# Second shift of the adaLN modulation without GpSimd: half of it on VectorE, half as modulation pieces on TensorE

## Chip, core and metric

One core of a Trainium2 chip. The time is device microseconds of one execution. TensorE, VectorE, ScalarE and GpSimd each run their own queue of instructions in order; SP (SyncE) issues most of the DMAs. TensorE's clock has two levels, 1.2 and 2.4 GHz; the profile gives the granted clock of a stretch as a share of the higher one.

## What is computed

One layer of a hybrid diffusion backbone on 384 tokens (128 context, 256 latent), D = 2048, everything in float32. What matters here is the modulation: six vectors per stream out of one condition vector each.

```python
sh1, sc1, g1, sh2, sc2, g2 = split(silu(cond) @ w_mod + b_mod, 6)   # cond: c_ctx and c
h = x * (1 + sc1) + sh1
# attention (q, k, v), Conformer convolution (width 31, then LayerNorm), Mamba-2 scan; all out of h @ w_in
x = layer_norm(ALPHA * x + g1 * (concat(A, B, C) @ w_out))
h2 = x * (1 + sc2) + sh2
x = layer_norm(ALPHA * x + g2 * conv_ffn(h2))
```

The second shift `sh2` is a product of a 2 x 2048 matrix with a 2048 x 2048 part of `w_mod`, 16.8 MB. It is needed only after the first LayerNorm.

## The kernel before

Each large matmul runs as three products of a high and a low part. `wpiece` (L219) takes a 512 KB weight piece into ring `raw` (4 buffers), casts its high part on ScalarE (L229) and subtracts for the low part on VectorE (L230). `load` (L213) issues from SP's queue. Instructions with a high priority are placed ahead by the scheduler, but each engine's queue stays in order.

The run has stages. Up to about 220 us: the first modulation and the first part of the input projection. Then a stage whose TensorE order is written out by hand: `phase_zd`, `phase_v`, eight head pairs of `qk_tile`, and the first 512 columns of the output projection (`wo_group` with 0). A planner, `flow`, interleaves small generators with these main matmuls. It keeps a clock of its own, in units meant as microseconds: main matmuls advance it through `tick`; a generator yields two numbers, how far its own TensorE work advances the clock, and after which pause it is due again. `tick` also issues taps of the width-31 convolution on VectorE from a list (`flow.bg`), as many as `flow.rate` times the main units pay for, 0.63 units each. When the main matmuls need a result that no generator has reported as ready, `advance` sets the planner's clock to the next generator's due time, so that no main matmul is issued in between.

The generators: `tok_gen`, `dt_gen` and `ssm_gen` (the scan), `attn_gen` (attention: scores, softmax on VectorE and ScalarE, transposes at L717, values), `conv_ln_gen` (LayerNorm behind the convolution, when the taps are done), `mod2_gen` (first gate and second scale: 64 pieces of 512 KB into ring `v`, 3 buffers, four matmuls of 32 output rows each into one PSUM bank, in batches of three with a pause of 11.5), and `sh2_gen` (second shift, one piece every 9 units from the end of the scan on).

A piece of the second shift (`sh2_piece`, L845) loads 512 KB into ring `raw`, the transposed weights with the output channel on the partition. There are 32 pieces, four quarters of K (`kq`) times eight pairs of output blocks. Odd ones go to `dve_gemv`: one VectorE instruction per half piece and stream multiplies with the broadcast condition row and accumulates. Even ones go to `pool_gemv`: GpSimd multiplies (L842) and ScalarE's copy accumulates (L843). At each new quarter `cond_rows` has GpSimd's queue issue two broadcast loads.

Behind the hand-ordered stage, the output projection's columns 1 to 3 run (three calls of `wo_group`); after each weight piece `sh2_piece` is called until all 32 are done. `mix_rows` and `gate` issue residual rows and gates from GpSimd's queue; `mix_evac` (L925) reads PSUM on VectorE and so frees it. `sh2_end` sums the partial sums in `macc` into `h2b`; the first LayerNorm `ln1` reads them. Then the FFN follows.

Of the kernel before, what the change touches and what calls it, by code (L numbers as in the profile page):

```python
# [15 lines left out]
KC = 16  # L16
# [83 lines left out]
def _build(tc, ctx, a):  # L100
# [112 lines left out]
    def load(src, n, raw=None):  # L213
        raw = raw_t() if raw is None else raw
        with tc.high_priority(offset=HP):
            nc.sync.dma_start(out=raw[:, :n], in_=src)
        return raw
# [250 lines left out]
    def dt_gen():  # L468
        e, u, d, m = s_t(48), s_t(48), s_t(48), s_t(48)
        V.scalar_tensor_tensor(out=e, in0=dtr, scalar=-1.0, in1=dtr, op0=ALU.mult, op1=ALU.min)  # L470
        S.activation(out=e, in_=e, func=AF.Exp)
        V.tensor_scalar_add(out=u, in0=e, scalar1=1.0)
        V.tensor_scalar_add(out=d, in0=u, scalar1=-1.0)
        V.tensor_scalar(out=m, in0=d, scalar1=0.0, scalar2=None, op0=ALU.is_equal)
        V.tensor_tensor(out=d, in0=d, in1=m, op=ALU.add)
        V.reciprocal(out=d, in_=d)
        S.activation(out=u, in_=u, func=AF.Ln)
        V.tensor_tensor(out=u, in0=u, in1=d, op=ALU.mult)
        V.tensor_tensor(out=u, in0=u, in1=m, op=ALU.add)
        V.tensor_tensor(out=u, in0=u, in1=e, op=ALU.mult)  # L480
        V.scalar_tensor_tensor(out=dtv, in0=dtr, scalar=0.0, in1=u, op0=ALU.max, op1=ALU.add)
        ea = s_t(16)
        S.activation(out=ea, in_=P_("a_log", 0, 16), func=AF.Exp)
        V.tensor_scalar(out=ea, in0=ea, scalar1=-1.0, scalar2=None, op0=ALU.mult)
        V.tensor_tensor(out=dA.rearrange("p (c d) -> p c d", c=3), in0=dtv.rearrange("p (c d) -> p c d", c=3),
                        in1=bc(ea, 1, 3), op=ALU.mult)
        yield 0.0, 9.0
        ps = at_t()
        dAv = dA.rearrange("p (c d h) -> p c d h", c=3, d=2)
        csv = cs.rearrange("p (c d h) -> p c d h", c=3, d=2)  # L490
        for d_, tri in ((0, tri_f), (1, tri_b)):
            PE.matmul(ps[:, 32 * d_:32 * d_ + 24], tri, dAv[:, :, d_, :])
            V.tensor_copy(out=csv[:, :, d_, :], in_=ps[:, 32 * d_:32 * d_ + 24].rearrange("p (c h) -> p c h", c=3))
        yield 0.5, 2.0
        PE.matmul(ps[:, 64:112], ones, dA)
        pt = at_t()
        PE.transpose(pt[:48, :128], cs, ident)
        ct = sbt([128, 128], "o", 1)
        V.tensor_copy(out=ct[:48, :], in_=pt[:48, :128])
        G.dma_start(out=csd, in_=ct[:48, :])  # L500
        V.tensor_scalar(out=ncs, in0=cs, scalar1=-1.0, scalar2=None, op0=ALU.mult)
        S.activation(out=eT, in_=ps[:, 64:112], func=AF.Exp)
        V.tensor_tensor(out=dec, in0=ps[:, 64:112], in1=cs, op=ALU.subtract)
        S.activation(out=dec, in_=dec, func=AF.Exp)
        S.activation(out=ecs, in_=cs, func=AF.Exp)
        yield 0.3, 0.0
        ready.add("dt")
# [251 lines left out]
    def mod2_start(g):  # L759
        gS[g] = gm_t()  # L760

    def mod2_load(i):
        g, half, k = i // 32, i // 16 % 2, i % 16
        return load(a["wm2"][g, half, k], 1024, v_t().rearrange("p a b -> p (a b)"))

    def mod2_piece(i, raw):
        g, half, k = i // 32, i // 16 % 2, i % 16
        for j in range(4):
            PE.matmul(gS[g][32 * j:32 * j + 32, 256 * half:256 * half + 256], cond[:, k, :],
                      raw[:, 256 * j:256 * j + 256], start=k == 0, stop=k == KC - 1)  # L770

    gd = {}
    s2 = sbt([128, KC, 2], "s2", 1)
# [2 lines left out]
    def mod2_end(g):  # L776
        ps = gS.pop(g)
        sm = gb_t()[:, :512]
        if g == 0:
            bg = gb_t()[:, :512]  # L780
            pinned(bg, a["bgate"])
            with tc.high_priority(offset=HP):
                V.tensor_tensor(out=sm, in0=ps, in1=bg, op=ALU.add)
            gd[g] = dr.tile([2, D], F32, tag=f"gd{g}", name=nm("gd"))
            for j in range(4):
                G.dma_start(out=gd[g][:, 512 * j:512 * j + 512], in_=sm[32 * j:32 * j + 2, :])
            return
        V.tensor_copy(out=sm, in_=ps)
        yield 0.0, 2.0
        pt = at_t()  # L790
        for b in range(4):
            PE.transpose(pt[:, 128 * b:128 * b + 128], sm[:, 128 * b:128 * b + 128], ident)
        pv = pt.rearrange("p (b j c) -> p j b c", b=4, j=4)[:, :, :, 0:2]
        V.tensor_tensor(out=s2.rearrange("p (j b) c -> p j b c", j=4), in0=pv,
                        in1=bc(b2p.rearrange("p (j b) -> p j b", j=4), 3, 2), op=ALU.add)
        yield 0.5, 1.0

    def mod2_gen(most, gap):
        i = 0
        while i < 64:  # L800
            n = min(most, 32 - i % 32)
            raws = [mod2_load(j) for j in range(i, i + n)]
            yield 0.0, gap
            if i % 32 == 0:
                mod2_start(i // 32)
            for j, raw in enumerate(raws):
                mod2_piece(i + j, raw)
            i += n
            yield 0.45 + 0.43 * n, 0.0
            if i % 32 == 0:  # L810
                yield from mod2_end(i // 32 - 1)

    macc = sbt([128, 32, 4], "macc", 1)
    cbc = []
# [19 lines left out]
        for e in range(2):  # L834
            dve_gemv(raw[:, 512 * e:512 * e + 512], 2 * pr + e, kq)

    sh2_done = [0]

    def pool_gemv(w, kt, kq):
        for s in range(2):  # L840
            j = m_t()
            G.tensor_tensor(out=j, in0=w, in1=cbc[s], op=ALU.mult)  # L842
            S.activation(out=j, in_=j, func=AF.Copy, accum_out=macc[:, 16 * s + kt, kq:kq + 1])  # L843

    def sh2_piece():  # L845
        i = sh2_done[0]
        if i == 32:
            return
        sh2_done[0] += 1
        kq, pr = i // 8, i % 8  # L850
        if pr == 0:
            cond_rows(kq, m_t)
        raw = load(a["wsh2"][kq, pr], 1024)
        for e in range(2):
            (dve_gemv if i % 2 else pool_gemv)(raw[:, 512 * e:512 * e + 512], 2 * pr + e, kq)

    def sh2_gen(gap):
        while "ssm" not in ready:
            yield 0.0, 1.0
        while "stop" not in ready:  # L860
            sh2_piece()
            yield 0.0, gap

    def sh2_end():
        m = s_t(32)
        V.tensor_reduce(out=m, in_=macc, axis=AX.X, op=ALU.add)
        V.tensor_tensor(out=h2b.rearrange("p k s -> p s k"), in0=m.rearrange("p (s k) -> p s k", s=2),
                        in1=bc(P_("bsh2", 0, 16), 1, 2), op=ALU.add)

    def g2_end():  # L870
        m = s_t(32)
# [90 lines left out]
    with tc.manual_schedule(engines={mybir.EngineType.PE}):  # L962
        for i in range(8):
            do_conv5(i)
        for i in range(4):
            flow.bg += conv31_steps(i)
        flow.rate = 0.7
        flow.add(30.0, tok_gen())
        flow.add(0.0, mod2_gen(3, 11.5))
        flow.add(40.0, conv_ln_gen())  # L970
        flow.add(30.0, ssm_gen())
        flow.add(50.0, attn_gen())
        flow.add(60.0, sh2_gen(9.0))
        phase_zd()
        flow.add(0.0, dt_gen())
        phase_v()
        for hp in range(8):
            k = qk_tile(0, hp)
            qk[hp] = (qk_tile(1, hp), k)
        ps = [mm_t() for _ in range(3)]  # L980
        for k in ORDER[:12]:
            cat_split(k)
        wo_group(0, ps, cat_split, lambda last: flow.tick(2.09))
        ready.add("stop")
        flow.drain()
        gb = mix_rows(0)
        for t in range(3):
            mix_evac(t, 0, 0, 512, ps[t], gb)
# [47 lines left out]
    for cg in range(1, 4):  # L1036
        gb = mix_rows(cg)
        ps = [ps_t() for _ in range(3)]
        wo_group(cg, ps, lambda k: None, lambda last: sh2_piece() if last else None)
        for t in range(3):  # L1040
            mix_evac(t, cg, 0, 512 if cg < 3 else 256, ps[t], gb)
    sh2_end()
    LW = 256
    lhi = [t_t(LW, F32R) for _ in range(KC)]
# [179 lines left out]
def _layout(i):  # L1224
# [3 lines left out]
    d = {}  # L1228
# [8 lines left out]
    for q, (k0, nk) in enumerate(PARTS):  # L1237
        w1 = wm[:, :, [1, 0], 128 * k0:128 * (k0 + nk)]
        kpl = 4 // nk
        d[f"wm1_{q}"] = f(w1.reshape(KC // kpl, kpl, 128, 256 * nk).transpose(0, 2, 1, 3).reshape(KC // kpl, 128, 1024))  # L1240
    d["wm2"] = f(wm[:, :, [2, 4]].reshape(KC, 128, 2, 4, 2, 256).transpose(2, 4, 0, 1, 3, 5).reshape(2, 2, KC, 128, 1024))
    for n, c in (("wsh2", 3), ("wg2", 5)):
        g2 = i["w_mod"][0][:, c * D:(c + 1) * D].T.reshape(8, 2, 128, 4, 512)
        d[n] = f(g2.transpose(3, 0, 2, 1, 4).reshape(4, 8, 128, 1024))
# [75 lines left out]
```

## Time and profile before

| | us |
|---|---|
| median of 3 runs | 1890.98 (1887.93 to 1893.52) |
| the profiled execution | 1888.23, span 1886.5 |
| TensorE busy | 1811.3 |
| VectorE busy | 1186.7 |
| ScalarE busy | 816.1 |
| GpSimd busy | 148.9 |
| mean granted TensorE clock | 0.985 |

TensorE is busy for 96% of the span. Idle time of another engine costs nothing by itself; what counts is what ended an idle stretch of TensorE, and whom that engine had waited for in turn. Times are counted from the span's start.

### The profile page before, as it was taken

Reading aid. Unit: us, or ns where it says so; the run is one execution under the profiler, and the core shown is the slowest. Engines: PE = TensorE matmul, PEld = TensorE weight load, DVE = VectorE, ACT = ScalarE, POOL = GpSimd, SP = SyncE. Lnnn points to the kernel's source line nnn. Section 1 sums busy time; section 2 is a strip of 40 time slices with the busy share of each in tenths; the row PEclk is TensorE's granted clock in tenths of the full one; section 3 lists DMA queues with packets and bytes.
Section 4 is the critical chain, followed back from the end, with each engine's and each line's share of the span. In section 5 each row is a group of like instructions: output and inputs, shape, how many; then the busy total and the mean of one; then the engine's idle time right before and its main releaser. Section 6 shows DMA issues by size and latency. Waiting matters only on the chain. (4 is left out here: it accounts for less than half of the span.)

```text
span 1886.5 us, 28860 instructions
## 1 busy us (share of the span) xinstructions
PE 1811.3 (96%) x10794; PEld 1635.4 (87%) x10794; DVE 1186.7 (63%) x2457; ACT 816.1 (43%) x1606; POOL 148.9 (8%) x213
## 2 busy tenths in 40 slices
PE   8999999989989888999999999999999999999998
PEld 6888988768776667999988999988999988999987
DVE  3865899944454567666743666744666644667567
ACT  4223543665655445644433444432444432444434
POOL 0000001110323452000000000000000000000000
PEclk9999999999989999999999999999999999999999
DMA  8898467656655765244444455444544544454354
GB/s 316 309 323 287 148 224 248 210 185 206 235 203 179 232 197 203 90 140 140 151 134 131 149 169 166 157 124 130 171 157 147 167 123 130 156 167 151 118 147 144
DMA packets 108652, 337.76 MB, mean 179 GB/s; under 512 B 12584, under 2 KB 17160, under 8 KB 108512
## 3 DMA queue, kind: packets, MB, share of 16 engines
q1 hardware_dynamic: 101280, 311.65, 50.5%
q0 software_dynamic: 7232, 24.28, 4.3%
q8 instruction: 84, 1.38, 0.3%
q14 instruction: 56, 0.46, 0.1%
HBM read 331.08 MB, written 4.79 MB: 178 GB/s over the span
## 5 line engine op out<-in xcount | busy, mean ns | idle before, releaser
L230 DVE TENSOR_TENSOR wlo<-raw,whi 128x512 fp32r<-128x512 f32 (+1 forms) x755 | 528.0, 701 | 483.2 <-ACT whi L229 476.1
L229 ACT CAST whi<-raw 128x512 fp32r<-128x512 f32 (+1 forms) x755 | 466.4, 620 | 843.2 <-PE mm L455 303.3
L454 PE MATMUL mm<-hl,whi 128*128 128x384 f32 x1245 | 429.0, 345 | 1.4 <-ACT whi L229 1.1
L455 PE MATMUL mm<-hl,whi 128*128 128x384 f32 x1245 | 422.6, 339 | 0.0
L456 PE MATMUL mm<-hl,wlo 128*128 128x384 f32 x1245 | 421.7, 339 | 0.0
L454 PEld LDWEIGHTS mm<-hl,whi 128*128 128x128 f32 x1245 | 236.0, 190 | 11.9 <-issue 5.7
L455 PEld LDWEIGHTS mm<-hl,whi 128*128 128x128 f32 x1245 | 236.1, 190 | 0.6 <-DVE wlo L230 0.2
L456 PEld LDWEIGHTS mm<-hl,wlo 128*128 128x128 f32 x1245 | 236.1, 190 | 0.0
L454 PE MATMUL sc<-hl,whi 128*128 128x384 f32 x659 | 222.8, 338 | 0.0
L455 PE MATMUL sc<-hl,whi 128*128 128x384 f32 x659 | 221.9, 337 | 0.0
L456 PE MATMUL sc<-hl,wlo 128*128 128x384 f32 x659 | 221.7, 336 | 0.0
L454 PEld LDWEIGHTS sc<-hl,whi 128*128 128x128 f32 x659 | 123.6, 188 | 2.9 <-ACT whi L229 1.6
L455 PEld LDWEIGHTS sc<-hl,whi 128*128 128x128 f32 x659 | 123.7, 188 | 0.1
L456 PEld LDWEIGHTS sc<-hl,wlo 128*128 128x128 f32 x659 | 123.7, 188 | 0.0
L826 DVE SCALAR_TENSOR_TENSOR junk<-raw,gb 128x512 bf16<-128x512 f32 x128 | 87.6, 684 | 50.2 <-DMA raw<-wg 50.1
L448 PE MATMUL mm<-whi,hl 128*128 128x512 f32 (+2 forms) x293 | 104.1, 355 | 7.7 <-DVE g L925 4.8
L449 PE MATMUL mm<-wlo,hl 128*128 128x512 f32 (+2 forms) x293 | 101.8, 347 | 2.3 <-DVE wlo L230 2.3
L450 PE MATMUL mm<-whi,hl 128*128 128x512 f32 (+2 forms) x293 | 101.3, 346 | 0.0
L842 POOL TENSOR_TENSOR m<-raw,m 128x512 f32<-128x512 f32 x64 | 86.7, 1383 | 117.9 <-DMA raw<-wsh 94.4
L450 PE MATMUL mm<-whi,t 128*128 128x512 f32 (+1 forms) x232 | 89.7, 387 | 0.0
L449 PE MATMUL mm<-wlo,t 128*128 128x512 f32 (+1 forms) x232 | 89.6, 386 | 0.0
L448 PE MATMUL mm<-whi,t 128*128 128x512 f32 (+1 forms) x232 | 89.5, 386 | 0.0
(354 smaller groups left out, 2592.6 us busy)
## 6 DMA issues: line engine op xcount, KB each, us to landing
raw<-wu SPq DMA_DIRECT2D x176, 512.0 KB, 3.5
raw<-wd SPq DMA_DIRECT2D x79, 512.0 KB, 3.7
m<-wm SPq DMA_DIRECT2D x128, 256.0 KB, 5.6
v<-wm SPq DMA_DIRECT2D x64, 512.0 KB, 6.1
raw<-wA SPq DMA_DIRECT2D x32, 512.0 KB, 5.5
raw<-wqk SPq DMA_DIRECT2D x32, 512.0 KB, 4.2
raw<-wsh SPq DMA_DIRECT2D x32, 512.0 KB, 4.3
raw<-wo SPq DMA_DIRECT2D x32, 512.0 KB, 4.4
```

The costliest lines, as they stand in the source:

```text
L229: S.copy(out=hi[:, :w], in_=rw)
L230: V.tensor_tensor(out=lo[:, :w], in0=rw, in1=hi[:, :w].bitcast(F32), op=ALU.subtract)
L448: PE.matmul(ps[:, :n], A, hi[:, w0:w0 + n], start=k == 0, stop=False)
L449: PE.matmul(ps[:, :n], A, lo[:, w0:w0 + n], start=False, stop=False)
L450: PE.matmul(ps[:, :n], B, hi[:, w0:w0 + n], start=False, stop=k == last)
L454: PE.matmul(ps[:, :T], A, hh[k], start=k == k0, stop=False)
L455: PE.matmul(ps[:, :T], A, hl[k], start=False, stop=False)
L456: PE.matmul(ps[:, :T], B, hh[k], start=False, stop=k == k1)
L826: V.scalar_tensor_tensor(out=j, in0=w, scalar=1.0, in1=cbc[s], op0=ALU.mult, op1=ALU.mult, accum_out=macc[:, 16 * s + kt, kq:kq + 1])
L842: G.tensor_tensor(out=j, in0=w, in1=cbc[s], op=ALU.mult)
```

## The change

The second shift's first half of K (quarters 0 and 1) stays on VectorE, in 32 steps of one output block and one quarter each: `sh2_load` takes 256 KB into ring `m`, and the condition rows with the first of a quarter; `sh2_step` computes the step at the head of a queue and issues the next load. Three loads are issued before the first step. The second half of K becomes 16 more pieces of `mod2_gen` (a third accumulation group, `wm3`), whose end writes `h2b` with the bias; `sh2_end` adds VectorE's half. GpSimd's products and ScalarE's accumulating copies are gone. Four numbers of the planner change: the pause of `mod2_gen` from 11.5 to 9, that of the second shift from 9 to 4 per step, `dt_gen`'s first pause from 9 to 14, and the taps' rate from 0.7 to 0.45.

```diff
-        yield 0.0, 9.0
+        yield 0.0, 14.0
...
+    def mod2_of(i):
+        return (i // 32, i // 16 % 2, i % 16, 0) if i < 64 else (2, (i - 64) // 8, 8 + i % 8, 8)
     def mod2_load(i):
-        g, half, k = i // 32, i // 16 % 2, i % 16
-        return load(a["wm2"][g, half, k], 1024, v_t().rearrange("p a b -> p (a b)"))
+        g, half, k, _ = mod2_of(i)
+        src = a["wm2"][g, half, k] if g < 2 else a["wm3"][half, k - 8]
+        return load(src, 1024, v_t().rearrange("p a b -> p (a b)"))
...
-        V.tensor_tensor(out=s2.rearrange("p (j b) c -> p j b c", j=4), in0=pv,
-                        in1=bc(b2p.rearrange("p (j b) -> p j b", j=4), 3, 2), op=ALU.add)
+        dst, bias = (s2, b2p) if g == 1 else (h2b, P_("bsh2", 0, 16))
+        V.tensor_tensor(out=dst.rearrange("p (j b) c -> p j b c", j=4), in0=pv,
+                        in1=bc(bias.rearrange("p (j b) -> p j b", j=4), 3, 2), op=ALU.add)
...
-        while i < 64:
-            n = min(most, 32 - i % 32)
+        while i < 80:
+            n = min(most, 32 - i % 32, 80 - i)
...
-    def pool_gemv(w, kt, kq):
-        for s in range(2):
-            j = m_t()
-            G.tensor_tensor(out=j, in0=w, in1=cbc[s], op=ALU.mult)
-            S.activation(out=j, in_=j, func=AF.Copy, accum_out=macc[:, 16 * s + kt, kq:kq + 1])
...
-        raw = load(a["wsh2"][kq, pr], 1024)
-        for e in range(2):
-            (dve_gemv if i % 2 else pool_gemv)(raw[:, 512 * e:512 * e + 512], 2 * pr + e, kq)
+    def sh2_load():
+        i = sh2_n[0]
+        if i == 32:
+            return
+        sh2_n[0] += 1
+        kq, kt = i // 16, i % 16
+        w = m_t()
+        with tc.high_priority(offset=HP):
+            nc.sync.dma_start(out=w, in_=a["wsh2"][kq, kt // 2, :, 512 * (kt % 2):512 * (kt % 2) + 512])
+        rows = None
+        if kt == 0:
+            rows = [m_t() for _ in range(2)]
+            for s in range(2):
+                G.dma_start(out=rows[s], in_=crow[s:s + 1, 512 * kq:512 * kq + 512].to_broadcast([128, 512]))
+        sh2_q.append((w, kt, kq, rows))
+
+    def sh2_step():
+        if sh2_q:
+            w, kt, kq, rows = sh2_q.pop(0)
+            if rows:
+                cbc[:] = rows
+            dve_gemv(w, kt, kq)
+        sh2_load()
...
+        for _ in range(3):
+            sh2_load()
+            yield 0.0, gap
         while "stop" not in ready:
-            sh2_piece()
+            sh2_step()
             yield 0.0, gap
...
-        flow.rate = 0.7
+        flow.rate = 0.45
-        flow.add(0.0, mod2_gen(3, 11.5))
+        flow.add(0.0, mod2_gen(3, 9.0))
-        flow.add(60.0, sh2_gen(9.0))
+        flow.add(60.0, sh2_gen(4.0))
...
-        wo_group(cg, ps, lambda k: None, lambda last: sh2_piece() if last else None)
+        wo_group(cg, ps, lambda k: None, lambda last: sh2_step() if last else None)
...
+    while sh2_q:
+        sh2_step()
     sh2_end()
```

## Rows read from the trace of the kernel before

**Rows 1.** The page, busy time: engine, us, share of the span, instructions.

```profile
PE 1811.3 (96%) x10794; PEld 1635.4 (87%) x10794; DVE 1186.7 (63%) x2457; ACT 816.1 (43%) x1606; POOL 148.9 (8%) x213
```

**Rows 2.** By stretch: length, PE, PEld, DVE, ACT, POOL busy, granted clock, DMA share, GB/s.

```profile
190.00:780.00 590.00, 532.54 (x3443) 451.90 (x3442) 404.38 (x864) 318.13 (x755) 131.50 (x162) 0.96 0.60 199
```

**Rows 3.** TensorE's waits, 270:290 us: who for whom, sum in us, times, longest.

```profile
PE at L492 <- issue: 3.4, 1, 3.4
PE at L492 <- DVE cs L493: 0.3, 1, 0.3
```

**Rows 4.** TensorE's waits, 480:545 us.

```profile
PE at L717 <- ACT p L707: 4.5, 3, 2.7
PE at L717 <- ACT t L603: 3.3, 1, 3.3
```

**Rows 5.** TensorE's waits, 600:630 us.

```profile
PE at L717 <- ACT t L733: 4.8, 2, 2.6
PE at L717 <- ACT p L707: 2.6, 2, 1.9
```

**Rows 6.** TensorE's waits, 650:741 us, the four largest.

```profile
PE mm L448 <- DVE g L925: 4.8, 1, 4.8
PE sc L448 <- DVE g L925: 3.6, 1, 3.6
PE mm L448 <- ACT whi L229: 2.7, 2, 1.5
PE mm L449 <- DVE wlo L230: 2.3, 4, 1.6
```

**Rows 7.** By stretch, columns as in rows 2.

```profile
280.00:300.00 20.00, 18.74 (x95) 14.65 (x96) 17.96 (x39) 5.02 (x11) 1.09 (x2) 0.91 0.52 172
600.00:640.00 40.00, 32.60 (x145) 23.46 (x144) 21.08 (x45) 18.93 (x47) 19.32 (x24) 0.87 0.71 224
700.00:720.00 20.00, 13.38 (x55) 10.73 (x54) 11.74 (x23) 9.51 (x23) 10.32 (x10) 0.83 0.59 202
```

**Rows 8.** In order of time, 658:670 us (four engines); last, ScalarE's wait, 460:740.

```profile
661.51 5.11 POOL L842 TENSOR_TENSOR m<-raw,m 128x512 f32<-128x512 f32 x4 [4.93 <-DMA raw<-wsh]
666.05 0.60 ACT L229 CAST whi<-raw 128x512 fp32r<-128x512 f32 x1
666.68 0.69 DVE L230 TENSOR_TENSOR wlo<-raw,whi 128x512 fp32r<-128x512 f32 x1 [4.95 <-ACT whi L229]
667.90 0.69 DVE L925 TENSOR_TENSOR g<-sc,gb 128x512 f32<-128x512 f32 x1
668.64 0.80 PE L448 MATMUL sc<-whi,hl 128*128 128x512 f32 x1 [3.56 <-DVE g L925]
...
ACT m L843 <- POOL m L842: 53.8, 40, 4.4
```

**Rows 9.** Groups of TensorE by line, 190:600 us: busy, mean ns, idle before.

```profile
L769 PE MATMUL gm<-v,cond 128*32 128x256 f32 x512 | 32.2, 383 | 0.0
L792 PE MATMUL at<-cons,gb 128*128 128x128 f32 x4 | 0.7, 286 | 1.4 <-DVE gb L788 1.4
```

**Rows 10.** Tile v's landing; SP's issue of one batch; a TensorE wait, whole span.

```profile
DMA to landing us min/median/max: 3.6/6.1/9.8
448.14 1.37 SPq L216 DMA_DIRECT2D v<-wm  x3
PE gm L280 <- DMA m<-wm: 7.7, 4, 4.4
```

**Rows 11.** By stretch, columns as in rows 2.

```profile
260.00:380.00 120.00, 112.49 (x756) 93.60 (x754) 113.53 (x230) 60.04 (x143) 13.53 (x22) 0.99 0.65 223
380.00:460.00 80.00, 71.69 (x488) 59.90 (x484) 37.52 (x79) 50.09 (x120) 9.69 (x17) 0.94 0.55 181
300.00:400.00 100.00, 94.91 (x671) 80.32 (x669) 84.31 (x165) 52.70 (x134) 16.12 (x27) 1.00 0.68 230
```

**Rows 12.** TensorE's waits, 400:470 us.

```profile
PE at L717 <- ACT p L707: 7.1, 2, 4.7
```

More of the change, by code (lines that the diff above doesn't have):

```diff
@@ L760, in mod2_start @@
         gS[g] = gm_t()
+    def mod2_of(i):
+        return (i // 32, i // 16 % 2, i % 16, 0) if i < 64 else (2, (i - 64) // 8, 8 + i % 8, 8)
     def mod2_load(i):
-        g, half, k = i // 32, i // 16 % 2, i % 16
-        return load(a["wm2"][g, half, k], 1024, v_t().rearrange("p a b -> p (a b)"))
+        g, half, k, _ = mod2_of(i)
+        src = a["wm2"][g, half, k] if g < 2 else a["wm3"][half, k - 8]
+        return load(src, 1024, v_t().rearrange("p a b -> p (a b)"))
     def mod2_piece(i, raw):
-        g, half, k = i // 32, i // 16 % 2, i % 16
+        g, half, k, k0 = mod2_of(i)
         for j in range(4):
             PE.matmul(gS[g][32 * j:32 * j + 32, 256 * half:256 * half + 256], cond[:, k, :],
-                      raw[:, 256 * j:256 * j + 256], start=k == 0, stop=k == KC - 1)
+                      raw[:, 256 * j:256 * j + 256], start=k == k0, stop=k == KC - 1)
     gd = {}
@@ L809, in mod2_gen @@
             yield 0.45 + 0.43 * n, 0.0
-            if i % 32 == 0:
-                yield from mod2_end(i // 32 - 1)
+            if i in (32, 64, 80):
+                yield from mod2_end((i - 1) // 32)
     macc = sbt([128, 32, 4], "macc", 1)
@@ L835, in g2_piece @@
             dve_gemv(raw[:, 512 * e:512 * e + 512], 2 * pr + e, kq)
-    sh2_done = [0]
-    def pool_gemv(w, kt, kq):
-        for s in range(2):
-            j = m_t()
-            G.tensor_tensor(out=j, in0=w, in1=cbc[s], op=ALU.mult)
-            S.activation(out=j, in_=j, func=AF.Copy, accum_out=macc[:, 16 * s + kt, kq:kq + 1])
-    def sh2_piece():
-        i = sh2_done[0]
+    sh2_q = []
+    sh2_n = [0]
+    def sh2_load():
+        i = sh2_n[0]
         if i == 32:
             return
[L849 to L852, printed above, removed]
-        raw = load(a["wsh2"][kq, pr], 1024)
-        for e in range(2):
-            (dve_gemv if i % 2 else pool_gemv)(raw[:, 512 * e:512 * e + 512], 2 * pr + e, kq)
+        sh2_n[0] += 1
[16 more added lines that the diff above has]
+        sh2_load()
     def sh2_gen(gap):
@@ L865, in sh2_end @@
         m = s_t(32)
-        V.tensor_reduce(out=m, in_=macc, axis=AX.X, op=ALU.add)
-        V.tensor_tensor(out=h2b.rearrange("p k s -> p s k"), in0=m.rearrange("p (s k) -> p s k", s=2),
-                        in1=bc(P_("bsh2", 0, 16), 1, 2), op=ALU.add)
+        V.tensor_reduce(out=m, in_=macc[:, :, 0:2], axis=AX.X, op=ALU.add)
+        hp_ = h2b.rearrange("p k s -> p s k")
+        V.tensor_tensor(out=hp_, in0=hp_, in1=m.rearrange("p (s k) -> p s k", s=2), op=ALU.add)
     def g2_end():
@@ L1241, in _layout @@
     d["wm2"] = f(wm[:, :, [2, 4]].reshape(KC, 128, 2, 4, 2, 256).transpose(2, 4, 0, 1, 3, 5).reshape(2, 2, KC, 128, 1024))
+    d["wm3"] = f(wm[8:, :, 3].reshape(8, 128, 4, 2, 256).transpose(3, 0, 1, 2, 4).reshape(2, 8, 128, 1024))
     for n, c in (("wsh2", 3), ("wg2", 5)):
```

## Prediction, made before the changed kernel was run

> **What bounds the kernel now.** I read the page first, then the waits of TensorE, then single stalls in order of time. TensorE is busy 1811.3 of 1886.5 us [rows 1], so only two things can move the end: matmul work, and TensorE's idle time with the clock that it costs. The 75 us of idle time don't lie evenly. The up and down projections from about 780 us on run at full width; most of it lies between 190 and 780 us, in the hand-ordered stage and the output projection: TensorE is busy there for 532.6 of 590 us, at a mean clock of 0.96 [rows 2]. There the listing in order of time and the waits by stretch show four clusters that the change can reach: 3.4 and 0.3 us where the dt matmul comes [rows 3]; 3.3 and 4.5 us at attention transposes between 480 and 545 us [rows 4]; 4.8 and 2.6 us at the last attention step, 600 to 630 us [rows 5]; 4.8, 3.6, 2.7 and 2.3 us in output columns 1 to 3, 650 to 741 us [rows 6]. Behind these stalls the granted clock falls below 1.00: 0.91 in the 20 us behind the first (and as much behind the second and behind the 3.6 us of the fourth), 0.87 over 40 us around the third, 0.83 around the 4.8 us of the fourth [rows 7]. A mean of 0.91 over 20 us is a part of the stretch at 1.2 instead of 2.4 GHz; it costs 0.09 x 20 = 1.8 us of full-speed work. I count it as a part of the stall.
>
> What makes the stalls of the fourth cluster is seen in one chain [rows 8]: GpSimd starts four products of the second shift at 661.51 us, when their tile has landed; ScalarE's accumulating copies stand in its queue behind them, so the weight's high part is cast only at 666.05; VectorE's low part follows at 666.68 and the eviction that frees the PSUM bank at 667.90; TensorE starts again at 668.64, 3.6 us late. Over the stage ScalarE stood 53.8 us before these copies, 40 times [rows 8]. The engines have room; their queues are in order, and one late tile holds three of them.
>
> **Parts that take time away.** (a) dt_gen's pause grows from 9 to 14 planner units (one unit is meant as 1 us). The planner puts 5 us more main matmuls ahead of the dt matmul, against 3.7 us of waiting, and the taps ahead of the dt chain on VectorE become sparser. I take the whole: 3.7 + 1.8 of clock = 5.5 us; bounds 0 and 5.5.
>
> (b) and (d) GpSimd's 64 products and ScalarE's 64 copies go. VectorE keeps 64 products (32 steps x 2 streams, before 16 pieces x 4), but in single steps, on tiles requested three steps earlier, out of ring m and no longer out of ring raw, which also holds every weight piece. So the queue chain above has no first link, and the weight loads behind a raw tile that GpSimd held are free too. For (b), 480 to 545 us, 3.3 + 4.5 + 1.8 of clock = 9.6 us; bounds 3 and 9.6, since an attention transpose also waits for exponentials that stay. For (d), 4.8 + 3.6 + 2.7 + 2.3 = 13.4, with 0.09 x 20 + 0.17 x 20 = 5.2 of clock, is 18.6; I leave 1.6 for refilling at three group starts and take 17; bounds 8 and 18.6. The planner's own additions say how much second shift reaches this place: before, 12 of 32 pieces are issued in the ordered stage and 20 in the three groups (8 + 8 + 4); after, with a pause of 4 for 9, 21 of 32 steps come earlier, 8 lie in the first group, 3 in the second, none in the third.
>
> (c) The last attention step. Adding up the planner's units: main matmuls are 32 x 1.09 + 16 x 2.09 + 256 x 0.522 + 16 x 2.09 = 235.4, and before, they reach head pair 7 at unit 350.7 while its attention ends at 357.5; the planner jumps ahead with nothing to issue. The trace has that as 7.4 us of idle and 0.13 x 40 = 5.2 of clock [rows 5, 7], 12.6 in all. After, the 16 new pieces push the main matmuls back and attention 7 ends at 354.2 with 10 units of output projection left, so something is there to issue. I take 10, since waits for single exponentials stay; bounds 3 and 12.6.
>
> Together 5.5 + 9.6 + 17 + 10 = 42.1 us.
>
> **Parts that add.** (e) 16 pieces on TensorE: the 64 pieces now take 32.2 us of engine time [rows 9], so 16 x 32.2 / 64 = 8.05 us, on the path, since TensorE is the bound. (f) One more mod2_end: four transposes, 0.7 us, and by the existing one a wait of 1.4 us for VectorE's copy [rows 9]: 2.1 us. Its two VectorE instructions and the one addition in sh2_end lie beside matmuls. (g) Denser modulation: batches of three come after a pause of 9 instead of 11.5, and there are 28 instead of 22. All three v buffers are in use, so a batch's load is issued only when the previous batch's matmuls have run. It lands 6.1 us after issue in the median, 9.8 at worst, and the third load is issued about 1 us after the first [rows 10]; by its additions the planner leaves 9.3 to 10.9 units. So most are hidden and the worst come about 1 us late: 2 us, bounds 0 and 34 (below). These loads stand on SP's queue, and weight loads behind one that waits for its buffer wait too; against that, ring raw holds four pieces.
>
> (h) The taps' rate falls from 0.7 to 0.45. By the planner the last tap comes at unit 272 instead of 154, so VectorE is less crowded than its 113.5 of 120 us at first and more than its 37.5 of 80 us later [rows 11]: 124 taps of 0.63 units over 272 units add 29%, about 76% in all. What crowding costs is bounded by the stretch where it is worst: TensorE idles 5.1 us in 300 to 400 us [rows 11]. At 0.64 of the density, over 118 units more, 5.1 / 100 x 118 x 0.64 = 3.9, less 1.8 at the first place. I take 4; bounds 0 and 8. The last tap meets the second shift's first step at unit 266, so the two crowds hardly overlap. The conv LayerNorm moves with the taps; its stall of 7.1 us at 416 us [rows 12] I move unchanged.
>
> GpSimd's queue keeps only DMA issues: the four row broadcasts (eight before), the biases, gates and residual rows no longer stand behind products. SP issues as many bytes as before, 32 loads of 256 KB and 16 of 512 KB instead of 32 of 512 KB. A load of 512 KB lands in 9.8 us at worst [rows 10]; three steps ahead is 12 units or more, so I cost these at nothing. If that cover failed, VectorE would stand before them in its queue, with splits and evictions behind it, and every us of it would reach TensorE as in the chain above.
>
> The Trainium skill speaks against this split: its page "DMA: Bandwidth & Descriptors", section "Bandwidth", wants transfers of 1 MiB or more, and its fixed 2.0 us plus bytes / 436 GB/s makes an estimated 2.6 us of 256 KB and 3.2 us of 512 KB, so 32 x 2.6 + 16 x 3.2 - 32 x 3.2 = 32 us more of queue occupancy. By the rows that occupancy is hidden and the sum keeps its value; by the page alone it could be at most those 32 us later.
>
> Sum: 8.05 + 2.1 + 2 + 4 = 16.2 added, 42.1 taken away, net -25.9. Against the profiled execution, 1888.23 us with a span of 1886.5, that is 1862.3; the median of the runs is 1890.98, 2.75 above it, so I forecast **1865 us**.
>
> **Rivals.** R1, slower: the modulation's v loads become the bound. In the first modulation TensorE did wait for such loads, 7.7 us in 4 waits [rows 10]. If the third load of each batch lands as late as the worst one now, 1.0 + 9.8 against 9.6 units of usable pause, 28 batches lose some 1.2 us each, 34 us, and the time is 1899. It decides once landing passes about 8.6 us after issue in the typical batch. Against it: not one of the 22 batches now waited [rows 9]. R2: the taps and the LayerNorm, moved among the steps of the second shift and attention, stall TensorE twice, 7.1 us once more and (h) at 8: 1865 + 11 = 1876. For it: that stage's exponentials already come last in most of its waits. R3, the change doesn't free what it means to free: behind the copies the weight loads, or the exponentials themselves, are late anyway, and half of (b), (c) and (d) stays: 18.3 us, 1883. For it: the casts also wait for landing weights now; against it, these weights share their ring and queue with the tiles that GpSimd holds.
>
> **How the numbers follow.** Chances: forecast 0.57, R2 0.17, R3 0.11, R1 0.15. With every bound at its best end (46.3 taken, 8.8 added, and the LayerNorm's 7.1 gone) the time is 1846; the upper end leaves out most of R1: 1846 to 1890. A measurement of this kernel tells about 0.3%, 5.7 us, from no change. Faster by more: forecast, R2 and part of R3, 0.77; within: 0.10; slower: 0.13.
>
> **What would show it.** Right: no idle time of TensorE ended by evictions in output columns 1 to 3, ScalarE with no wait for GpSimd, granted clock 1.00 from 600 to 720 us, the dt stall gone, the modulation's matmuls up by 8 us, none of them behind a DMA. Wrong: waits for v tiles (R1); attention transposes idle for ScalarE's exponentials between 400 and 600 us in sum more than now (R2); casts waiting for weights in the output groups (R3).

## The result and the profile after

| | before | after |
|---|---|---|
| median, us | 1889.45 (1887.25 to 1893.52) | 1834.11 (1833.33 to 1837.13) |
| profiled span, us | 1886.5 | 1835.3 |
| TensorE idle in the span, us | 75.2 | 36.0 |
| mean granted clock | 0.985 | 0.994 |

The ratio is 0.9708, 95% interval 0.9686 to 0.9729: 55 us less, where 1865 was forecast and 1846 was the lower end of the range. The direction was right, the size less than half of what came, and the time lies outside the range.

Cut the run at four places that both kernels have: the last evacuation of `phase_zd`, the last query tile, the first eviction of the output projection, the first cast of the LayerNorm's result. First the kernel before, then after; columns as in rows 2.

```profile
264.80:566.10 301.30, 273.41 (x1859) 229.53 (x1858) 198.15 (x426) 170.24 (x424) 54.46 (x69) 0.95 0.63 212
566.10:629.80 63.70, 55.00 (x305) 39.44 (x304) 29.20 (x72) 34.31 (x91) 25.41 (x29) 0.92 0.60 189
629.80:753.20 123.40, 105.28 (x552) 87.71 (x551) 86.76 (x185) 55.91 (x132) 49.98 (x42) 0.96 0.65 212
```

```profile
264.70:561.30 296.60, 279.85 (x2013) 231.50 (x2011) 227.76 (x532) 165.41 (x402) 30.91 (x51) 0.97 0.75 261
561.30:603.90 42.60, 42.60 (x251) 32.12 (x250) 17.88 (x40) 20.39 (x49) 7.95 (x15) 1.00 0.66 205
603.90:702.80 98.90, 98.90 (x561) 86.04 (x560) 58.75 (x111) 35.67 (x69) 3.75 (x7) 1.00 0.52 156
```

The value, key and query stage is 4.7 us shorter, the last attention step with the first output columns 21.1, the other output columns 24.5. What lies behind took 1133.3 and 1132.5 us, what lies ahead 264.8 and 264.7. The second and third stretch now have no idle time of TensorE at all and a clock of 1.00; where rows 5 and 6 showed 7.4 us and 13.4 us of listed waits there is nothing left. The second stretch is not the same work before and after: some of its main matmuls and attention now lie in the first.

In the first stretch waits remain, and not fewer where I had expected that. TensorE's waits, 474 to 548 us, after (answers to rows 4):

```profile
PE at L717 <- ACT p L707: 4.8, 3, 3.2
PE at L717 <- ACT t L603: 0.9, 1, 0.9
PE at L599 <- DVE m L595: 0.6, 1, 0.6
PE at L717 <- ACT pt L719: 0.6, 1, 0.6
PE at L717 <- ACT g L385: 0.4, 1, 0.4
```

They sum to 7.3 us, against 7.8 in rows 4. The next two answers suggest why; no run tests it alone: the second shift's products on VectorE (ns min/median/max, first and last start), and a stretch in which VectorE is nearly full (columns as in rows 2).

```profile
L831 DVE SCALAR_TENSOR_TENSOR junk<-m,m x64: 671/691/694, 474.6 to 547.3; 128x512 bf16<-128x512 f32 x64
```

```profile
500.00:540.00 40.00, 35.05 (x235) 27.09 (x235) 38.58 (x108) 24.52 (x55) 2.66 (x5) 0.94 0.92 330
```

All 32 steps ran within 73 us, as soon as the scan was done and the tiles had landed. The planner's places fix the order on TensorE alone; VectorE's instructions and the loads are placed by the scheduler, which took them early. None was left for the output columns. The kernel without second shift (below) has only 3.9 us of waits at these transposes, so about half of the 7.8 us was the second shift's, and the changed kernel did not win it.

### The profile page after: what moved, and what is told of

It is laid out like the page before. It is cut to its first block, busy times and chain, and to the rows that moved or that the text cites. A ratio compares the mean times of both kernels' runs of the same rounds, so it can differ in the third digit from the quotient of the medians.

```text
span 1835.3 us, 28924 instructions
## 1 busy us (share of the span) xinstructions
PE 1799.3 (98%) x10926; PEld 1628.6 (89%) x10926; DVE 1179.0 (64%) x2459; ACT 777.4 (42%) x1477; POOL 61.1 (3%) x145
## 5 line engine op out<-in xcount | busy, mean ns | idle before, releaser
L230 DVE TENSOR_TENSOR wlo<-raw,whi 128x512 fp32r<-128x512 f32 (+1 forms) x755 | 521.3, 691 | 471.8 <-ACT whi L229 468.8
L448 PE MATMUL mm<-whi,hl 128*128 128x512 f32 (+2 forms) x293 | 101.2, 346 | 0.1
L450 PE MATMUL mm<-whi,hl 128*128 128x512 f32 (+2 forms) x293 | 99.4, 339 | 0.0
L358 DVE SCALAR_TENSOR_TENSOR t<-g,par,t 128x399 f32<-128x399 f32 x120 | 75.2, 650 | 0.9
```

Of the source, the lines that this page charges most:

```text
L230: V.tensor_tensor(out=lo[:, :w], in0=rw, in1=hi[:, :w].bitcast(F32), op=ALU.subtract)
L358: V.scalar_tensor_tensor(out=cvo[i][:, :399], in0=glu[i][:, j:j + 399], scalar=P_("conv_w", 31 * i + j), in1=cvo[i][:, :399], op0=ALU.mult ...
L448: PE.matmul(ps[:, :n], A, hi[:, w0:w0 + n], start=k == 0, stop=False)
L450: PE.matmul(ps[:, :n], B, hi[:, w0:w0 + n], start=False, stop=k == last)
```

## Experiments

Ratios are against the kernel before, run beside each. "Before with" and "changed with" name the kernel that was edited.

| kernel | median, us | ratio (95%) |
|---|---|---|
| before, no second shift | 1833.59 | 0.9695 (0.9680 to 0.9709) |
| before, without GpSimd's half | 1836.85 | 0.9711 (0.9696 to 0.9726) |
| before, tiles ahead | 1888.51 | 0.9982 (0.9973 to 0.9991) |
| before, no copies | 1902.30 | 1.0069 (1.0054 to 1.0084) |
| before, tiles ahead and no copies | 1885.01 | 0.9962 (0.9948 to 0.9975) |
| ... and GpSimd scaling one tile | 1851.62 | 0.9786 (0.9757 to 0.9815) |
| ... and GpSimd filling zeros | 1849.85 | 0.9781 (0.9757 to 0.9805) |
| before, copies without products | 1855.83 | 0.9813 (0.9796 to 0.9830) |
| before, all products on VectorE | 1857.76 | 0.9820 (0.9800 to 0.9840) |
| before, taps' rate 0.45 | 1872.61 | 0.9898 (0.9882 to 0.9915) |
| changed, taps' rate 0.7 | 1831.90 | 0.9693 (0.9679 to 0.9708) |
| changed, dt pause 9 | 1834.20 | 0.9704 (0.9690 to 0.9719) |
| changed, step pause 9 | 1835.45 | 0.9711 (0.9697 to 0.9726) |
| changed, without the 16 pieces | 1828.39 | 0.9676 (0.9660 to 0.9692) |
| changed, rate 0.7, modulation pause 11.5 | 1861.22 | 0.9849 (0.9834 to 0.9864) |
| changed, all on VectorE, 0.7 and 11.5 | 1831.72 | 0.9692 (0.9677 to 0.9706) |
| changed, all on VectorE, 0.45 and 9 | 1829.55 | 0.9667 (0.9650 to 0.9683) |

### What the second shift cost in the kernel before

```diff
     def sh2_piece():
+        return
```

> The kernel before with the second shift's product left out (no loads, no products, zeros in their place): the price of the second shift in the kernel before. The stretch from the end of the query and key tiles to the first LayerNorm took 63.7 us (last columns of the ordered stage) and 123.4 us (output columns 1 to 3); in the changed kernel 42.6 and 98.9. Theory Q (the second shift's tiles, products and copies stand in the queues of GpSimd, ScalarE and SP in front of the weights' work): nearly all of the gain is the removal of this, so the time is 1835 or below, with columns 1 to 3 at 99 us. Theory M (metering: rate of the taps and pauses decide): columns 1 to 3 get shorter, but the stalls between 400 and 560 us stay, time about 1855.

1833.59 us: the second shift cost 58 us, and the changed kernel, which does compute it, is as fast as the kernel before without it. The three stretches (columns as in rows 2):

```profile
266.20:554.20 288.00, 268.10 (x1858) 225.57 (x1858) 185.36 (x395) 160.17 (x390) 26.51 (x45) 0.97 0.60 203
554.20:603.50 49.30, 49.30 (x301) 36.69 (x301) 19.35 (x47) 25.66 (x62) 7.58 (x15) 1.00 0.52 165
603.50:701.30 97.80, 97.80 (x556) 85.19 (x556) 58.67 (x110) 35.57 (x70) 4.68 (x9) 1.00 0.51 168
```

There is no idle time in the latter two, though no new piece fills the planner's jump there. So the stalls of rows 5 and 6 all belonged to the second shift. The dt stall (3.4 us) and the 7.1 us near 416 us do not: they stand in this kernel as in the one before. Theory Q held on the time; how the second shift costs that was open.

```diff
+        if i % 2 == 0:
+            return
         raw = load(a["wsh2"][kq, pr], 1024)
         for e in range(2):
-            (dve_gemv if i % 2 else pool_gemv)(raw[:, 512 * e:512 * e + 512], 2 * pr + e, kq)
+            dve_gemv(raw[:, 512 * e:512 * e + 512], 2 * pr + e, kq)
```

> The kernel before without the half of the second shift that goes to GpSimd and ScalarE (that half is left out): VectorE's 16 pieces stay in the weights' ring. It divides the price of 58 us: if VectorE's half in this ring carries little, 1838 to 1843; if the late tiles in this ring carry half of it, 1855 to 1862, as where the copies or the products stood alone.

1836.85 us, just under the lower case's bounds: nearly the whole price, about 55 us, lay in the half that went through GpSimd and ScalarE. VectorE's half cost some 3 us (the intervals overlap), in the weights' ring and without any load ahead.

### Which link of GpSimd's half

```diff
-        raw = load(a["wsh2"][kq, pr], 1024)
-        for e in range(2):
-            (dve_gemv if i % 2 else pool_gemv)(raw[:, 512 * e:512 * e + 512], 2 * pr + e, kq)
+        w = m_t()
+        with tc.high_priority(offset=HP):
+            nc.sync.dma_start(out=w, in_=a["wsh2"][kq, kt // 2, :, 512 * (kt % 2):512 * (kt % 2) + 512])
...
+        sh2_q.append((w, kt, kq, rows))
...
+            w, kt, kq, rows = sh2_q.pop(0)
...
+            (dve_gemv if kt // 2 % 2 else pool_gemv)(w, kt, kq)
```

> The kernel before with one part of the change alone: the second shift's tiles come in single 256 KB steps into the ring of the products, requested three steps ahead, all of K; half the steps still go to GpSimd's products and ScalarE's copies. Theory Q in its first form (a late tile is the first link; it holds GpSimd, this ScalarE): with the tile there in time most of the stalls behind evictions go, 1855. Theory E (the products and copies themselves hold the queues: a product takes 1.3 us on GpSimd, and 64 copies of 0.8 us stand in ScalarE's queue in front of casts): only the weights' ring is relieved, 1875. Theory M: 1885 or above.

1888.51 us, three us less than before: Theory Q in its first form (1855) and E (1875) both missed, and M's number (1885 or above) came without M's reason. Tiles that are there in time free the output columns (97.7 us, like no second shift at all), but the two stretches ahead of them grow from 301.3 + 63.7 to 310.9 + 77.7 us: GpSimd's products, which started between 472.9 and 724.7 us, now all start between 475.4 and 636.1, and the price went with them. The chain of rows 8 was read rightly, but taking away its first link, the late tile, does not take away the price.

```diff
             G.tensor_tensor(out=j, in0=w, in1=cbc[s], op=ALU.mult)
-            S.activation(out=j, in_=j, func=AF.Copy, accum_out=macc[:, 16 * s + kt, kq:kq + 1])
```

> The kernel before without ScalarE's 64 accumulating copies; GpSimd's products stay (their sums, a half of the second shift, are left out). Which engine carries the price of 58 us that leaving out the whole second shift took away? If ScalarE's queue (copies in front of casts and exponentials, waiting for GpSimd): most of it goes, 1840 to 1850. If GpSimd itself (tiles of the weights' ring held through slow products, VectorE slowed beside it): 1870 or above.

1902.30 us: the second case (1870 or above), and slower than with the copies, which it had not named. SP stands before buffers of the weights' ring that GpSimd's products keep, 82.8 us here and 76.6 in the kernel before (460 to 760 us), and the casts wait for weights, 14.7 us between 460 and 740 us in the kernel before, here 71.0 (460 to 760 us; SP's own waits, then one of ScalarE's; for whom, sum in us, times, longest):

```profile
SPq L216 <- POOL m L843: 82.8, 15, 6.8
```

```profile
ACT whi L229 <- DMA raw<-wo: 71.0, 14, 12.2
```

So ring and copies looked like two holders of which either is enough. That was the next theory, and taking both away tests it. To the kernel with tiles ahead:

```diff
-            S.activation(out=j, in_=j, func=AF.Copy, accum_out=macc[:, 16 * s + kt, kq:kq + 1])
```

> The kernel before with the second shift's tiles three steps ahead in the products' ring and without ScalarE's 64 copies (GpSimd's sums, half of the second shift, are left out). Theory T (two holders, each enough alone: the weights' ring, whose buffers GpSimd's slow products keep and behind which SP's queue stands; and ScalarE's copies that wait for those products): with both taken away GpSimd's products cost nothing, 1835 to 1842. Theory G (GpSimd's products themselves slow the others, whatever waits for them): 1865 or above.

1885.01 us: Theory T fell too, and G (1865 or above) came: no copies, no shared ring, and the price still there. What is left of GpSimd's half is its products and their loads. Beside them VectorE is seen to stretch; in order of time in the kernel with tiles ahead, GpSimd first, then VectorE:

```profile
547.91 10.15 POOL L843 TENSOR_TENSOR m<-m,m 128x512 f32<-128x512 f32 x6
...
548.42 1.78 DVE L826 SCALAR_TENSOR_TENSOR junk<-m,m 128x512 bf16<-128x512 f32 x1
...
551.83 1.77 DVE L230 TENSOR_TENSOR wlo<-raw,whi 128x512 fp32r<-128x512 f32 x1
...
557.07 1.54 DVE L826 SCALAR_TENSOR_TENSOR junk<-m,m 128x512 bf16<-128x512 f32 x1
...
558.74 0.68 DVE L826 SCALAR_TENSOR_TENSOR junk<-m,m 128x512 bf16<-128x512 f32 x1
...
560.29 0.68 DVE L230 TENSOR_TENSOR wlo<-raw,whi 128x512 fp32r<-128x512 f32 x1
```

Until GpSimd's last product ends at 558.06 us the same instructions take up to two and a half times as long as behind it, and GpSimd's own take 10.15 / 6 = 1.69 us, where their median in the kernel before was 1.29. An attention transpose stood 14.2 us for its exponentials, behind this stretch and the casts for the output projection that follow it on ScalarE. It can be worse. In the kernel with tiles ahead and no copies six products ran at their full speed, 7.55 / 6 = 1.26 us, and the first of two splits beside them took 6.61 us; it ended 0.55 us behind the last of them:

```profile
588.40 7.55 POOL L844 TENSOR_TENSOR m<-m,m 128x512 f32<-128x512 f32 x6
589.89 7.22 DVE L230 TENSOR_TENSOR wlo<-raw,whi 128x512 fp32r<-128x512 f32 x2 [0.34 <-ACT whi L229]
```

The Trainium skill has this on its page "GPSIMD Engine Reference", section "1. Specifications": GpSimd's SBUF interface is shared with VectorE, with contention for VectorE's instructions with two SBUF inputs. The trace agrees: the splits and products that took 1.54 to 1.78 us above read two tiles.

Two more kernels keep tiles ahead and no copies, and change what GpSimd does:

```diff
-            G.tensor_tensor(out=j, in0=w, in1=cbc[s], op=ALU.mult)
+            G.tensor_scalar(out=j, in0=w, scalar1=2.0, scalar2=None, op0=ALU.mult)
```

> As the run with tiles ahead and without copies (1885), but GpSimd's 64 products of two tiles are replaced by 64 scalings of one tile by a constant (the second shift's half on GpSimd is left out so). Theory P (GpSimd's reads from SBUF hold VectorE's two-input instructions beside them): VectorE's split and product still stretch from 0.69 us to above 1 us in the mean, and the time follows the length of GpSimd's instructions: 1855 to 1885. If only GpSimd's instructions with two inputs hold VectorE: splits at 0.69 us, 1835 to 1840.

```diff
-            G.tensor_tensor(out=j, in0=w, in1=cbc[s], op=ALU.mult)
+            G.memset(j, 0.0)
```

> As the run with tiles ahead and without copies (1885), but GpSimd fills its 64 tiles with zeros instead of products: it reads nothing (the second shift's half on GpSimd is left out so). Theory P: nothing stretches on VectorE, 1835 to 1840. If any work of GpSimd on SBUF beside VectorE stretches it, its writes too: 1850 or above.

1851.62 and 1849.85 us. Splits by line, 466 to 660 us (count, busy us, mean ns, idle before): products of two tiles, scaling of one, zeros, and last the changed kernel.

```profile
L230 DVE TENSOR_TENSOR wlo<-raw,whi 128x512 fp32r<-128x512 f32 x46 | 54.0, 1180 | 7.0 <-ACT whi L229 6.9
```

```profile
L230 DVE TENSOR_TENSOR wlo<-raw,whi 128x512 fp32r<-128x512 f32 x61 | 46.5, 764 | 24.7 <-ACT whi L229 24.2 <-PE mm L456 0.3
```

```profile
L230 DVE TENSOR_TENSOR wlo<-raw,whi 128x512 fp32r<-128x512 f32 x61 | 42.0, 689 | 30.1 <-ACT whi L229 29.3 <-DMA v<-wm 0.3
```

```profile
L230 DVE TENSOR_TENSOR wlo<-raw,whi 128x512 fp32r<-128x512 f32 x65 | 44.7, 690 | 54.0 <-ACT whi L229 53.8
```

GpSimd's products were as long as its scalings (1.56 and 1.64 us in the mean), so length is not it. Products with two inputs take splits from 0.69 to 1.18 us, a scaling with one to 0.76, and zeros, which read nothing, leave them at 0.69. Zero fills are short (0.53 us), so fewer VectorE instructions meet one; but of those that did, 13 splits and 16 of VectorE's own products, not one was longer than 0.69 us. The 30 splits and 58 products of VectorE beside a scaling took 0.84 and 0.88 us in the mean, the 17 and 36 beside a two-input product of GpSimd 2.02 and 1.47. GpSimd's reads do it, and a second input most of all. The time went from 1885 to 1852 us when the second input went, and to 1850 when the first went too. Where the time went is seen in the wait of attention transposes for their exponentials, from 466 us to the end of attention (652 and 620 us), first with products, then with scalings:

```profile
PE at L717 <- ACT p L707: 31.9, 6, 13.3
```

```profile
PE at L717 <- ACT p L707: 10.6, 4, 7.2
```

Neither expectation was met. With scalings, Theory P's splits above 1 us did not come, nor did the other case's 1835 to 1840 us. With zeros nothing stretched, as P had it, and the time was about that of the other case (1850 or above): 16 us over the kernel without second shift. VectorE waits 24.5 us for second shift tiles there, beside a modulation with the old pauses; no run tests this rest, and it stays open.

```diff
-            G.tensor_tensor(out=j, in0=w, in1=cbc[s], op=ALU.mult)
-            S.activation(out=j, in_=j, func=AF.Copy, accum_out=macc[:, 16 * s + kt, kq:kq + 1])
+            S.activation(out=j, in_=w, func=AF.Copy, accum_out=macc[:, 16 * s + kt, kq:kq + 1])
```

> The kernel before without GpSimd's products; ScalarE's 64 accumulating copies read the weight tile directly (their sums are not the second shift's). If the wait of a copy for GpSimd's product is what holds ScalarE's queue: 1845 to 1855. If the copies' own 64 x 0.82 = 52 us in that queue do it: 1870 or above.

```diff
-            (dve_gemv if i % 2 else pool_gemv)(raw[:, 512 * e:512 * e + 512], 2 * pr + e, kq)
+            dve_gemv(raw[:, 512 * e:512 * e + 512], 2 * pr + e, kq)
```

> The kernel before with all 128 products of the second shift on VectorE, tiles still in the weights' ring and requested when used; nothing on GpSimd and no copies on ScalarE. Theory E: the stalls through ScalarE go, though VectorE gets 64 x 0.77 = 49 us more work, 1860. Theory Q in its first form: the late tiles now hold VectorE directly, with splits and evictions behind them, so the stalls stay, 1885 to 1900. Theory M: 1885.

1855.83 us, the first case to within a microsecond, and 1857.76, near Theory E's 1860. Without GpSimd's products 34 us go, whether ScalarE's copies stay or VectorE takes the half, as long as the tiles lie in the weights' ring and are requested when used. The other 19 to 21 of the half's 55 us stay in both. With all products on VectorE, the own ring and the loads ahead are worth another 24 us by the ratios, at the same rate and modulation pause but with the changed kernel's two other pauses (1831.72, below): casts in the output columns then have their weights, for which they waited 40.9 us here.

What the 34 us are in the kernel before, the queue's waits or the stretching, no run separates. The three stretches of the kernel with copies and without products (columns as in rows 2):

```profile
266.00:561.00 295.00, 269.71 (x1858) 226.53 (x1858) 194.84 (x427) 171.82 (x430) 28.54 (x49) 0.95 0.65 218
561.00:612.80 51.80, 49.96 (x302) 36.70 (x302) 26.19 (x70) 31.73 (x85) 8.50 (x16) 1.00 0.66 220
612.80:720.50 107.70, 101.50 (x556) 87.69 (x555) 81.29 (x185) 53.72 (x135) 5.88 (x11) 0.97 0.74 245
```

VectorE has the same work there and is busy 302.3 us, in the kernel before, beside the products, 314.1: the stretching comes to 12 us. With tiles ahead and no copies it was busy 358.1 us, with zeros in the products' place 302.8: there it comes to 55.

### The metering

```diff
-        flow.rate = 0.7
+        flow.rate = 0.45
```

> The kernel before with the taps' rate alone changed, 0.7 to 0.45. Theory M: the dt stall (3.7 us) and the LayerNorm stall at 416 us (7.1 us, with 5 us of clock behind it) go without anything else, 1873. Theories Q and E: the taps now meet the second shift's work, and nothing of the chain behind the late tiles changes, 1885 to 1895.

1872.61 us, as Theory M had it: in the kernel before, the rate alone was worth 19 us. The dt stall fell from 3.4 to 1.2 us, the 7.1 us near 416 us to 2.1, and the two first stretches together from 365.0 to 336.3 us, but the output columns rose from 123.4 to 136.6.

```diff
-        flow.rate = 0.45
+        flow.rate = 0.7
```

> The changed kernel with the taps' rate put back to 0.7. Theory M: the LayerNorm stall (7.1 us of idle at 416 us before, and the lower clock behind it) comes back, and the small stalls of 300 to 400 us with it: 1845 to 1850. Theories Q and E: the gain lies in the second shift, the time stays within 4 us of 1834.

1831.90 us, within the interval of the changed kernel: there the rate is worth nothing, though 4.2 us of wait for exponentials come back, near 410 us. Why it is worth 19 us in one kernel and nothing in the other stays open. The taps did not meet GpSimd's products: in the kernel before they start between 244.1 and 375.7 us, the products from 472.9 us on, and with the rate at 0.45 up to 447.1 and from 454.5 us on.

```diff
-        yield 0.0, 14.0
+        yield 0.0, 9.0
```

> The changed kernel with dt_gen's first pause put back from 14 to 9 units, the taps' rate at 0.45. If the pause removed the dt stall: 3.4 us of idle come back near 280 us, with 1.8 us of clock, 1839. If the sparser taps removed it: 1834, no stall there.

1834.20 us: no difference, with 0.6 and 0.8 us of waits at the dt matmul. With the rate at 0.7 and the pause at 14 they were 0.3 and 0.6. Each of the two alone takes most of the 3.7 us away.

```diff
-        flow.add(60.0, sh2_gen(4.0))
+        flow.add(60.0, sh2_gen(9.0))
```

> The changed kernel with the second shift's pause per step put back from 4 to 9 units, so that 19 to 20 of 32 steps (instead of 11) fall into output columns 1 to 3. Theory Q (late tiles): the tiles are there in time, so the place does not matter: 1834, columns 1 to 3 at 99 us. If the place matters (less of the second shift behind the evictions): columns 1 to 3 take 3 to 8 us longer, 1840.

1835.45 us, the same, and not a test of the place: the products ran from 473.7 to 547.3 us here too, by the scheduler's choice.

```diff
-        flow.rate = 0.45
+        flow.rate = 0.7
-        flow.add(0.0, mod2_gen(3, 9.0))
+        flow.add(0.0, mod2_gen(3, 11.5))
```

> The changed kernel with the taps' rate at 0.7 and the modulation's pause at 11.5, so with the two main metering numbers of the kernel before; second shift and dt pause as changed. If the metering carries a part of the gain: 1840 or above. If the second shift's move carries it all: 1830 to 1834.

1861.22 us, 29 more than with the rate at 0.7 alone. TensorE's waits from the last query tile to the first eviction:

```profile
PE gm L773 <- DMA v<-wm: 9.3, 8, 2.1
PE at L796 <- DVE gb L792: 0.8, 1, 0.8
```

28 batches of 11.5 + 1.74 units need 371, and by the planner's own count the changed kernel's stage ends at unit 366. The last batches come when no main matmul is left beside them, each behind its own load; the granted clock of the stretch is 0.86. So the shorter pause is what lets the 16 pieces hide. Without the pieces the old pause does no harm of this kind (1831.72 us with 0.7 and 11.5, below).

### The pieces on TensorE, and a faster version

```diff
-        while i < 80:
+        while i < 64:
```

> The changed kernel without the 16 modulation pieces on TensorE; the second half of K of the second shift is left out. The forecast's terms (e), (f) and (g): 8.05 + 2.1 + 2 = 12.2 us less, 1822. If the pieces cost their TensorE time and nothing else: 8.8 us less, 1825. If they fill idle time at the last attention step, as (c) has it: 1828 or above, with idle time back between 560 and 604 us.

1828.39 us, some 6 us less: the third case's time without its sign, since there is no idle time between 553.5 and 595.5 us. The pieces take 8.1 us of engine time (80 pieces 40.3 us, before 64 in 32.2), so 2 or so seem to lie in time that was idle.

The same without pieces, all 64 steps on VectorE:

```diff
-        if i == 32:
+        if i == 64:
             return
         sh2_n[0] += 1
...
-        flow.rate = 0.45
+        flow.rate = 0.7
-        flow.add(0.0, mod2_gen(3, 9.0))
+        flow.add(0.0, mod2_gen(3, 11.5))
```

> The changed kernel with the whole second shift on VectorE (64 steps, tiles three steps ahead, no pieces on TensorE), the taps' rate at 0.7 and the modulation's pause at 11.5. TensorE saves the 6 to 9 us of the 16 pieces; VectorE gets 64 x 0.77 = 49 us more. If VectorE's free room in the output columns takes it: 1826. If its crowd holds splits, softmax and evictions: 1840 or above.

And with the changed kernel's own rate and pause:

```diff
-        flow.rate = 0.7
+        flow.rate = 0.45
-        flow.add(0.0, mod2_gen(3, 11.5))
+        flow.add(0.0, mod2_gen(3, 9.0))
```

> The changed kernel with the whole second shift on VectorE, nothing on TensorE, the taps' rate at 0.45 and the modulation's pause at 9. TensorE saves 6 us of pieces; against 0.7 and 11.5 (1831.7) the dt stall of 2.5 us and a part of the stalls near 545 us should go: 1826 to 1829. If the crowd on VectorE decides: 1834 or above.

1831.72 us, between the two cases, and 1829.55, at the upper end of the first. With the whole second shift on VectorE, tiles ahead in their own ring and nothing on TensorE, the second of these beats the changed kernel, though narrowly: 0.9650 to 0.9683 against 0.9686 to 0.9729. VectorE has the room: in the output columns it is then busy 74.4 of 98.5 us, and TensorE still has no idle time there.

## Why the prediction was off

Every sign that the prediction gave for being right came: no idle time behind evictions in the output columns, no copy that waits for GpSimd (ScalarE's only waits for GpSimd, 4.5 us, lie in the scan), the dt stall at 0.3 us, a clock of 1.00 from 600 to 720 us, 8.1 us more of modulation matmuls and none behind a DMA. So what it said would go did go; the sizes were wrong. By stretch, with the costs in the first, it had 1.1 us more (5.5 + 9.6 - 16.2), 10 less and 17 less; the two profiled executions have 4.7, 21.1 and 24.5 less, 50.3 against 25.9.

- **(a) dt.** Right: 3.7 us of waits became 0.3. Two parts of the change do it, and each alone does most of it.
- **(b) attention transposes, 9.6 us.** Wrong in its place. The waits between 474 and 548 us sum to 7.3 us, against 7.8 of rows 4; VectorE has all 32 steps there, in 73 us, which the planner's count (11 of them later) did not foresee. The clock was mis-sized too: 1.8 us was one stretch of 20 us, but in the kernel before the granted clock is 0.91, 0.96 and 0.84 in 480 to 500, 520 to 540 and 540 to 560 us, 5.8 us. What did get smaller in this stage is what I moved unchanged: the 7.1 us near 416 us; 4.7 us of other waits remain near 420 us, behind the scan's output.
- **(c) last attention step, 10 us.** The size was short (idle 8.7 us to none, clock 0.92 to 1.00, the stretch 21.1 us shorter, some of it main work and attention that now lie earlier) and the reason was wrong: the planner's jump costs nothing when the exponentials come in time, as two kernels without pieces show.
- **(d) output columns, 17 us.** Mechanism right, size short: 24.5. I summed the four largest waits, 13.4 us, and took off 1.6 for refilling; the whole idle time of the stretch was 18.1 us, the clock about 5 more, and nothing of either remained.
- **The costs, 16.2 us.** (e) 8.05 was 8.1 of engine time; (e) to (g) together cost some 6 us, not 12.2, with no wait at the new transposes (L796) and none for a v tile. (h) cost nothing that can be told. The 32 us of queue occupancy, which the sum left out, did not show either: VectorE waited 4.8 us in all for second shift tiles between 474 and 548 us. The fit behind them is one that the Trainium skill's page "DMA: Bandwidth & Descriptors" gives for DMAs issued by GpSimd (section "Anatomy of one DMA — SWDGE (gpsimd) path"), and SP issued these.
- **The failing step.** The terms (c) and (d) were sums of the listed waits of a few clusters, with clock from windows around them and something taken off for caution. All idle time and all clock loss of the three stretches were 54.7 + 25 = 80 us in the kernel before; the clusters held 46.3 of it. The kernel without second shift shows what (b) to (d) should have been: its three stretches sum to 435.1 us against 488.4, so 53 us, where the forecast took 36.6. On the other side, the costs (e) to (h) were about 10 us too high.
- **What the prediction had no term for.** Each product on GpSimd made VectorE's splits beside it longer: in the kernel before, 54 splits averaged 776 ns between 466 and 660 us, against 690 after. This is inside TensorE's idle time before, so it does not by itself explain the short sum, and there it is 12 us of VectorE's time. It does explain why the chain's links could not be taken away one by one: when a wait was removed (tiles ahead, copies) the products ran closer together and the stretching took the place of the wait. The change removes GpSimd's products whole, so the forecast came out in the right direction without knowing this.
- **Rivals.** R1 didn't happen: no wait for v tiles, at 5.6 us from issue to landing. R2's sign did not come: the transposes' wait for exponentials between 400 and 600 us fell from 15.5 to 6.2 us. R3 was refuted: the casts of the output projection's weights wait 2.6 us for them in all.

Idle time in the three stretches fell from 54.7 to 16.8 us and the clock's loss from about 25 to 9: 54 us, less 8.7 of new matmuls, is 45, against 50.3 measured. Clocks rounded to 0.01 and modelled matmul ends leave some 5 us without a place.

## What to carry to other kernels

Before pricing an engine's removal, sum all idle time and all clock loss of the stretches that it touches, and not the largest waits alone. Compare, too, the same instruction's duration in stretches with and without that engine: a slow helper may cost time where no wait names it. A background job in an in-order machine did best here with its own ring and loads some steps ahead, so that neither the main loads nor the main casts stood behind it; with GpSimd's products still there, the same ring and loads gained 3 us. And whoever adds batches to a metered job has to shorten its pause, or the tail comes when nothing covers it.

## What the runs showed of the hardware

Beside GpSimd's two-input float32 products, VectorE's two-input instructions of 128 x 512 mostly took up to 1.8 us instead of 0.69, and one of them 6.61 (mean 2.02 for the 17 splits beside a product in the kernel with tiles ahead and no copies); beside one-input scalings 0.84 (splits) and 0.88 (VectorE's products) in the mean, beside zero fills 0.69. GpSimd's products slowed as well, from a median of 1.29 us in the kernel before to one of 1.71 with tiles ahead. Taking ScalarE's copies off the kernel before made it slower by 0.69%.
